# The first FFN chunks' low weight halves on VectorE instead of GpSimd, and half of the last layer norm's first token block on VectorE

## The chip, the core and the metric

The kernel runs on one core of one Trainium2 chip. A core has TensorE (PE, matmuls into eight PSUM banks), VectorE (DVE), ScalarE (ACT), GpSimd (POOL) and SyncE (SP, which here issues nearly all DMAs). Each engine works through its own instructions in a fixed order and waits on semaphores for what others deliver. The metric is the time of one execution in microseconds, the median of several.

## The reference

One decoder block, 512 tokens of 1024 channels, fp32: three sub-layers, each with its input shifted and scaled, and its output gated, by vectors computed from a conditioning vector c; each ends in a layer norm over the residual sum.

```python
mod = (silu(c) @ w_ada + b_ada).reshape(9, D)
sh1, sc1, g1, sh2, sc2, g2, sh3, sc3, g3 = mod
u = x * (1 + sc1) + sh1
x = layer_norm(ALPHA * x + g1 * (0.5 * swiglu(u, w_gu1, w_down1)), ln1_g, ln1_b)
u = x * (1 + sc2) + sh2
x = layer_norm(ALPHA * x + g2 * mixing(u), ln2_g, ln2_b)
u = x * (1 + sc3) + sh3
x = layer_norm(ALPHA * x + g3 * (0.5 * swiglu(u, w_gu2, w_down2)), ln3_g, ln3_b)
```

`swiglu` is `(silu(a) * g) @ w_down` with `a, g` the halves of `u @ w_gu` (2 x 2816 columns). `mixing` is stick-breaking attention beside a gated depthwise convolution. The change touches the start of the first FFN (`sc1`, `sh1`, `u`, and the first 8 of the 44 column tiles of `w_gu1`) and the last layer norm.

## The kernel before

Every fp32 matmul is done as three fp32r products: a matrix is split into a high part (a cast, `whi`, `uh`) and a low part (what the cast leaves, `wlo`, `ul`), and whi x uh, whi x ul and wlo x uh are summed in PSUM. Weights arrive as tiles of 128 x 1024 (512 KB). Such a tile is loaded into one of 3 slots named `raw`, ScalarE casts it to `whi` (L112), and another engine writes `wlo = raw - whi` (L113) into one of 5 slots; in most of the kernel that engine is GpSimd, in the down projections and two tiles of the second FFN it is VectorE. A slot of `raw` is free again when `wlo` is made, slots of `whi` and `wlo` when TensorE has read them.

The first FFN begins in `first_group`, because `u` is not there yet: the scale and shift vectors come from `silu(c) @ w_ada`. The loop runs over 8 chunks k of 128 input channels. Per chunk it loads one tile of x transposed (`xT`, 256 KB), four tiles of ada weights (256 KB each) and one `raw` tile (L100). VectorE multiplies each ada tile by `crow` (silu(c) on all partitions) and sums it along its columns in one instruction (`column_sums`, L188); reduces the four sums to a scale and a shift per channel, `m` (L448, L449). ScalarE makes `uf = xT * scale + shift` (L454; for k = 0 VectorE does, L452). VectorE casts `uf` to `uh` (L456) and subtracts for `ul` (L457). TensorE then does 8 x 3 matmuls of 128 x 512, one set of three for each of 8 PSUM banks (L460, L461, L464), where the eight banks hold the a and g halves of FFN columns 0 to 3. After chunk 7 the rest of the FFN follows, tiles h4a, h4g, h5a and so on, 24 matmuls each (L143 to L145), with their weights' `wlo` on GpSimd. Meanwhile VectorE works off background tasks in its gaps (further gate, scale and shift vectors, L188, L221).

A scheduler of the language decides the order of instructions on each engine from the order of the code and its own estimate of time; `keep_in_program_order` fixes the order among the instructions given to it. `load(..., True)` keeps the first loads in the order of the code on SP's queue. The loads of SP use eight semaphores in turn, so a load is issued only when the one eight places before it has landed.

The last layer norm (`layer_norm_out`) runs per block t of 128 tokens while TensorE still works on the later blocks. `residual_stats` adds PSUM and x (L260) and takes the statistics (L261, L263, L265) on VectorE, and GpSimd makes `rstd` (L267). The rest is done in one of two ways, for the last `dve_from` channels and for the others: ScalarE normalises (L334, with a bias `shift` from L333) and GpSimd multiplies by g and adds b (L335, L336); or VectorE does both in two instructions (L340, L341). `dve_from` is the number of channels that go the way of ScalarE and GpSimd: 1024 for t = 0, 512 for t = 1 and 2, none for t = 3.

Of the kernel before, what the change touches and what calls it, by code (L numbers as in the profile page):

```python
# [25 lines left out]
SEG = 2  # L26
# [16 lines left out]
def decoder_block(ctx: ExitStack, tc: tile.TileContext, a: dict, out: bass.AP):  # L43
    nc = tc.nc

    core = ctx.enter_context(tc.tile_pool(name="core", bufs=1))
    wts = ctx.enter_context(tc.tile_pool(name="wts", bufs=1))
# [16 lines left out]
    def bank(name, tag="ps"):  # L64
        return banks["pool"].tile([P, 512], F32, tag=tag, name=name, bufs=banks["bufs"][tag])
# [21 lines left out]
    b0pair = vec[:, 0:16].rearrange("p (c two) -> p c two", two=2)  # L87
# [11 lines left out]
    def load(dst, src, chain=False):  # L99
        ins = nc.sync.dma_start(dst, src).ins  # L100
        if "last" in issued:
            tc.add_manual_dep(ins, issued["last"].name,
                              mybir.DependencyInfo(mybir.DependencyClass.NoSync, mybir.DependencyReason.DATA),
                              reason="first loads in order of use")
        if chain:
            issued["last"] = ins


    def split_w(raw, lo_eng):
        hi = wts.tile([P, 1024], F32R, align_bytes=256, tag="whi", name="whi", bufs=5)  # L110
        lo = wts.tile([P, 1024], F32R, align_bytes=256, tag="wlo", name="wlo", bufs=5)
        nc.scalar.copy(hi, raw)  # L112
        lo_eng.tensor_sub(lo, raw, hi.bitcast(F32))  # L113
        return hi, lo

    def raw_tile(src, chain=False):
        raw = wts.tile([P, 1024], F32, tag="raw", name="raw", bufs=3)
        load(raw, src, chain)
        return raw
# [64 lines left out]
    def column_sums(parts, raw, crow):  # L184
        w = D // SEG
        for q in range(parts.shape[-1]):
            qs = slice(q * w, (q + 1) * w)
            nc.vector.scalar_tensor_tensor(raw[:, qs], raw[:, qs], 1.0, crow[:, qs], ALU.mult, ALU.mult,  # L188
                                           accum_out=parts[:, q : q + 1])
# [135 lines left out]
    def layer_norm_out(pool, t, banks_t, rows):  # L325
        r, mv, rstd = residual_stats(pool, t, banks_t)
        o = core.tile([P, D], F32, tag=f"x{t}", name="o")
        g, b = rows
        dve_from = {0: D, 1: 512, 2: 512}.get(t, 0)
        if dve_from:  # L330
            cs = slice(D - dve_from, D)
            shift = pool.tile([P, 1], F32, tag="shift", name="shift", bufs=2)
            nc.vector.scalar_tensor_tensor(shift, mv[:, 0:1], -1.0, rstd, ALU.mult, ALU.mult)  # L333
            nc.scalar.activation(o[:, cs], r[:, cs], AF.Identity, bias=shift, scale=rstd)  # L334
            nc.gpsimd.tensor_mul(o[:, cs], o[:, cs], g[:, cs])  # L335
            nc.gpsimd.tensor_add(o[:, cs], o[:, cs], b[:, cs])  # L336
            nc.sync.dma_start(out[t * P : (t + 1) * P, cs], o[:, cs])
        for c0 in range(0, D - dve_from, 512):
            cs = slice(c0, c0 + 512)
            nc.vector.scalar_tensor_tensor(o[:, cs], r[:, cs], mv[:, 0:1], g[:, cs], ALU.subtract, ALU.mult)  # L340
            nc.vector.scalar_tensor_tensor(o[:, cs], o[:, cs], rstd, b[:, cs], ALU.mult, ALU.add)  # L341
            nc.sync.dma_start(out[t * P : (t + 1) * P, cs], o[:, cs])
# [83 lines left out]
    crow = lnp.tile([P, D], F32, name="crow")  # L426
# [1 line left out]
    nc.gpsimd.dma_start(vec[:, 0 : 2 * KC], a["vecs"][:, 0 : 2 * KC])  # L428
    nc.scalar.activation(crow, crow, AF.Silu)
    b1 = core.tile([P, KC, 2], F32, name="b1")  # L430
    nc.vector.tensor_scalar_add(b1[:, :, 0:1], b0pair[:, :, 0:1], 1.0)
    nc.vector.tensor_copy(b1[:, :, 1:2], b0pair[:, :, 1:2])

    def first_group(gated, fp):
        pss = [bank(f"first{i}") for i in range(NFIRST)]
        uh, ul = u1
        for k in range(KC):
            parts = fp.tile([P, 2, SEG], F32, tag="parts0", name="parts0", bufs=2)
            xc = fp.tile([P, S], F32, tag="sF", name="xT", bufs=NF)
            load(xc, a["xT"][k], True)  # L440
            for x in range(2):
                for h in range(2):
                    rt = fp.tile([P, S], F32, tag="sF", name="ada0", bufs=NF)
                    hs = slice(h * 512, (h + 1) * 512)
                    load(rt, a["ada0"][k, x, :, hs], True)
                    column_sums(parts[:, x, h * SEG // 2 : (h + 1) * SEG // 2], rt, crow[:, hs])
            m = fp.tile([P, 2], F32, tag="m0", name="m0", bufs=2)
            nc.vector.tensor_reduce(m, parts, mybir.AxisListType.X, ALU.add)  # L448
            nc.vector.tensor_add(m, m, b1[:, k, :])  # L449
            uf = fp.tile([P, S], F32, tag="sF", name="uf0", bufs=NF)  # L450
            if k == 0:
                nc.vector.tensor_scalar(uf, xc, m[:, 0:1], m[:, 1:2], ALU.mult, ALU.add)  # L452
            else:
                nc.scalar.activation(uf, xc, AF.Identity, bias=m[:, 1:2], scale=m[:, 0:1])  # L454
            wh, wl = split_w(raw_tile(a["gu1_first"][k], True), nc.gpsimd)
            nc.vector.tensor_copy(uh[:, k, :], uf)  # L456
            nc.vector.tensor_sub(ul[:, k, :], uf, uh[:, k, :].bitcast(F32))  # L457
            for i, ps in enumerate(pss):
                cs = slice(i * P, (i + 1) * P)
                nc.tensor.matmul(ps, wh[:, cs], uh[:, k, :], start=(k == 0), stop=False)  # L460
                nc.tensor.matmul(ps, wh[:, cs], ul[:, k, :], start=False, stop=False)  # L461
# [32 lines left out]
    def begin1(gated, fp):  # L494
        return first_group(gated, fp)
# [483 lines left out]
```

## Time and profile before

| | us |
|---|---|
| median of 3 runs | 1330.25 (1327.76 to 1333.49) |
| the profiled execution | 1328.88 |
| its span (first to last instruction) | 1327.2 |
| first matmul of the first group | 11.37 |
| first matmul of h4a, behind the first group | 66.84 |
| TensorE busy | 1292.2 |
| VectorE, ScalarE, GpSimd busy | 750.8, 524.6, 559.7 |

The rows of the trace that are shown further down read: start in us from the span's start, duration in us, engine, line, operation, out<-in with their shapes, number of instructions in a row of the same kind, and in brackets how long the engine sat idle before it and what ended that wait. Matmuls overlap on TensorE, so that its pace is the distance between starts, not the duration. For VectorE and ScalarE too, the distance of starts is a little less than the duration when instructions follow each other directly.

### The profile page before, as it was taken

How to read it: one execution, taken by the hardware profiler on the slowest of the kernel's cores; microseconds unless marked ns; L12 is line 12 of the kernel's file. 1: busy time of each engine (PE TensorE's matmuls, PEld its weight loads, DVE VectorE, ACT ScalarE, POOL GpSimd, SP SyncE). 2: the span in 40 equal slices, each digit the busy share in tenths (PEclk: the TensorE clock that was granted, in tenths of full speed). 3: DMA queues.
4: the chain of work that ended last, by engine and by line, in shares of the span. 5: the costliest groups of instructions: out<-in, count | busy, mean ns of one | idle time of the engine just before them, and what ended most of it. 6: DMA issues, size and time to landing. Idle time of an engine off the chain costs nothing.

```text
span 1327.2 us, 16780 instructions
## 1 busy us (share of the span) xinstructions
PE 1292.2 (97%) x6444; PEld 1071.2 (81%) x6444; DVE 750.8 (57%) x1017; ACT 524.6 (40%) x794; POOL 559.7 (42%) x392
## 2 busy tenths in 40 slices
PE   6899999999999999999999999999999999999997
PEld 4688888888889878788778888878898888888885
DVE  7886885255462858766676876545672000025545
ACT  2233312222256555556556444852542222222220
POOL 2464535644222554534442111133264566564434
PEclk9999999999999989999999999999999999999999
DMA  9668886333327564655566989293273333323311
GB/s 356 217 211 314 293 293 215 103 96 96 95 81 171 123 150 96 159 112 118 121 135 135 191 193 200 51 225 109 77 272 100 101 106 101 117 96 96 96 64 63
DMA packets 57713, 197.36 MB, mean 149 GB/s; under 512 B 6673, under 2 KB 6817, under 8 KB 57633
## 3 DMA queue, kind: packets, MB, share of 16 engines
q1 hardware_dynamic: 47808, 160.63, 36.6%
q0 software_dynamic: 9824, 35.66, 16.4%
q8 instruction: 50, 0.82, 0.2%
q14 instruction: 31, 0.25, 0.1%
HBM read 194.17 MB, written 2.10 MB: 148 GB/s over the span
## 4 chain that ended last, share of the span: by engine, by line
PE 84%; DVE 8%; DMA 3%; issue 2%; ACT 1%; POOL 1%; SPq 0%; DVEq 0%; POOLq 0%; ACTq 0%
PE y L354 19%; DVE ada L188 3%; PE z L624 1%; DVE cacc L525 1%; PE pw L646 1%; PE glub L143 1%; PE ga L143 1%; PE ga L145 1%; PE ysb L145 1%; PE ga L144 1%; PE ysb L144 1%; PE ysb L143 1%; PE q L143 1%; PE glub L144 1%; PE glub L145 1%
## 5 line engine op out<-in xcount | busy, mean ns | idle before, releaser
L113 POOL TENSOR_TENSOR wlo<-raw,whi 128x1024 fp32r<-128x1024 f32 x88 | 224.8, 2561 | 239.0 <-ACT whi L112 233.5
L112 ACT CAST whi<-raw 128x1024 fp32r<-128x1024 f32 x144 | 149.6, 1046 | 265.3 <-DMA raw<-in_gu 45.2
L136 POOL TENSOR_TENSOR raw<-raw,mod_g 128x1024 f32<-128x1024 f32 x52 | 130.0, 2502 | 146.9 <-DMA raw<-in_dn 83.7
L525 DVE SCALAR_TENSOR_TENSOR cacc<-h,cv_w,cacc 128x512 f32<-128x512 f32 x232 | 179.7, 833 | 0.0
L129 ACT CAST whi<-raw 128x1024 fp32r<-128x1024 f32 x68 | 71.1, 1048 | 129.1 <-PE ysb L144 23.4
L113 DVE TENSOR_TENSOR wlo<-raw,whi 128x1024 fp32r<-128x1024 f32 x56 | 106.2, 1896 | 24.2 <-ACT whi L112 24.2
L354 PE MATMUL y<-whi,sh 128*128 128x512 f32 x352 | 113.8, 390 | 0.0
L354 PE MATMUL y<-wlo,sh 128*128 128x512 f32 x352 | 113.7, 389 | 0.0
L354 PE MATMUL y<-whi,sl 128*128 128x512 f32 x352 | 113.6, 389 | 0.0
L188 DVE SCALAR_TENSOR_TENSOR ada<-ada,crow 128x512 f32<-128x512 f32 x96 | 97.9, 1067 | 20.9 <-DMA ada<-in_ada_t 15.4
L418 DVE TENSOR_TENSOR sl<-sF,sh 128x512 fp32r<-128x512 f32 x44 | 45.3, 1031 | 85.3 <-ACT sh L417 85.3
L417 ACT CAST sh<-sF 128x512 fp32r<-128x512 f32 x44 | 27.1, 623 | 144.9 <-PE y L354 132.1
L131 POOL DMA_DIRECT2D wlo<-in_w_in x44 | 38.4, 872 | 98.9 <-ACT wlo L130 92.9
L636 POOL TENSOR_TENSOR be<-be,nb 128x127 f32<-128x127 f32 (+1 forms) x64 | 50.1, 783 | 68.7 <-DVE nb L631 55.1
L354 PEld LDWEIGHTS y<-whi,sl 128*128 128x128 f32 x352 | 66.1, 188 | 13.7
L354 PEld LDWEIGHTS y<-wlo,sh 128*128 128x128 f32 x352 | 66.1, 188 | 13.7
L354 PEld LDWEIGHTS y<-whi,sh 128*128 128x128 f32 x352 | 66.1, 188 | 13.5
L130 ACT ACTIVATE wlo<-whi 128x1024 fp32r<-128x1024 f32 x68 | 71.9, 1061 | 0.7
L650 DVE TENSOR_TENSOR wTl<-pw,wTh 128x128 fp32r<-128x128 f32 (+1 forms) x64 | 31.1, 485 | 52.8 <-ACT wTh L649 52.7
L634 POOL TENSOR_SCALAR_AFFINE_SELECT be<-be 128x128 f32<-128x128 f32 x64 | 40.9, 639 | 41.0 <-ACT be L630 40.6
L631 DVE TENSOR_TENSOR_SCAN nb<-nb,future 128x127 f32<-128x127 f32 (+1 forms) x64 | 53.4, 835 | 3.4 <-ACT nb L629 3.4
L221 DVE SCALAR_TENSOR_TENSOR acc<-ada,silu_c,acc 128x1024 f32<-128x1024 f32 x21 | 41.6, 1981 | 15.8 <-DMA ada<-in_ada_w 15.6
(494 smaller groups left out, 3376.4 us busy)
## 6 DMA issues: line engine op xcount, KB each, us to landing
raw<-in_gu SPq DMA_DIRECT2D x80, 512.0 KB, 3.6
raw<-in_w_in SPq DMA_DIRECT2D x48, 512.0 KB, 3.6
raw<-in_dn SPq DMA_DIRECT2D x44, 512.0 KB, 3.5
wlo<-in_w_in POOLq DMA_DIRECT2D x44, 512.0 KB, 6.0
ada<-in_ada_t SPq DMA_DIRECT2D x32, 512.0 KB, 5.3
ada<-in_ada_w SPq DMA_DIRECT2D x24, 512.0 KB, 5.0
ada<-in_ada SPq DMA_DIRECT2D x32, 256.0 KB, 6.0
raw<-in_gu_first SPq DMA_DIRECT2D x8, 512.0 KB, 6.6
```

The costliest lines, as they stand in the source:

```text
L112: nc.scalar.copy(hi, raw)
L113: lo_eng.tensor_sub(lo, raw, hi.bitcast(F32))
L129: nc.scalar.copy(hi, raw)
L130: nc.scalar.mul(lo, hi.bitcast(F32), -1.0)
L136: nc.gpsimd.tensor_mul(raw, raw, G)
L143: nc.tensor.matmul(ps[:, c0:c1], wh[:, ks], mov(uh, k)[:, c0:c1], start=(k == 0), stop=False)
L188: nc.vector.scalar_tensor_tensor(raw[:, qs], raw[:, qs], 1.0, crow[:, qs], ALU.mult, ALU.mult, accum_out=parts[:, q : q + 1])
L354: nc.tensor.matmul(acc[t][h][:, c0 - h * 512 : c1 - h * 512], st[:, tsl], wt[:, c0:c1], start=(k == 0 and i == 0 and c0 % 512 == 0), stop= ...
L418: nc.vector.tensor_sub(sl, sF[f], sh.bitcast(F32))
L525: ins = nc.vector.scalar_tensor_tensor(o, hv, cv_w[:, j, i : i + 1], o, ALU.mult, ALU.add)
L631: nc.vector.tensor_tensor_scan(nb[:, 1:n][:, ::-1], nb[:, 1:n][:, ::-1], future[:, S - n + 1 : S][:, ::-1], 1.0, ALU.mult, ALU.max)
L636: nc.gpsimd.tensor_mul(be[:, 0 : n - 1], be[:, 0 : n - 1], nb[:, 1:n])
```

## The change

In `first_group` the loop body is written anew. `wlo` of the eight chunks is made by VectorE (L473, and L477 for chunk 0) and no longer by GpSimd. The load of `raw` stands ahead of the four ada loads for k > 0. The cast to `whi` (L455) comes before the ada sums in the code and thereby before `uf` on ScalarE. `column_sums` is written out with one 512-column sum per tile, as before. All these instructions are given to `keep_in_program_order`. The two small instructions on `b1` move into the loop. The matmuls are unchanged. In `layer_norm_out`, `dve_from` for t = 0 is 512 and no longer 1024, as for t = 1 and 2.

```diff
-        dve_from = {0: D, 1: 512, 2: 512}.get(t, 0)
+        dve_from = {0: 512, 1: 512, 2: 512}.get(t, 0)
...
         for k in range(KC):
             parts = fp.tile([P, 2, SEG], F32, tag="parts0", name="parts0", bufs=2)
             xc = fp.tile([P, S], F32, tag="sF", name="xT", bufs=NF)
             load(xc, a["xT"][k], True)
+            raw = None if k == 0 else raw_tile(a["gu1_first"][k], True)
...
+            if k == 0:
+                raw = raw_tile(a["gu1_first"][k], True)
+            wh = wts.tile([P, 1024], F32R, align_bytes=256, tag="whi", name="whi", bufs=5)
+            wl = wts.tile([P, 1024], F32R, align_bytes=256, tag="wlo", name="wlo", bufs=5)
+            if k:
+                in_turn(nc.scalar.copy(wh, raw))
+            for x in range(2):
+                for h in range(2):
+                    rt = rts[2 * x + h]
+                    in_turn(nc.vector.scalar_tensor_tensor(rt, rt, 1.0, crow[:, h * 512 : (h + 1) * 512], ALU.mult,
+                                                           ALU.mult, accum_out=parts[:, x, h : h + 1]))
             m = fp.tile([P, 2], F32, tag="m0", name="m0", bufs=2)
-            nc.vector.tensor_reduce(m, parts, mybir.AxisListType.X, ALU.add)
-            nc.vector.tensor_add(m, m, b1[:, k, :])
+            in_turn(nc.vector.tensor_reduce(m, parts, mybir.AxisListType.X, ALU.add))
...
+            in_turn(nc.vector.tensor_add(m, m, b1[:, k, :]))
             uf = fp.tile([P, S], F32, tag="sF", name="uf0", bufs=NF)
             if k == 0:
-                nc.vector.tensor_scalar(uf, xc, m[:, 0:1], m[:, 1:2], ALU.mult, ALU.add)
+                in_turn(nc.vector.tensor_scalar(uf, xc, m[:, 0:1], m[:, 1:2], ALU.mult, ALU.add))
+                in_turn(nc.scalar.copy(wh, raw))
             else:
-                nc.scalar.activation(uf, xc, AF.Identity, bias=m[:, 1:2], scale=m[:, 0:1])
-            wh, wl = split_w(raw_tile(a["gu1_first"][k], True), nc.gpsimd)
-            nc.vector.tensor_copy(uh[:, k, :], uf)
-            nc.vector.tensor_sub(ul[:, k, :], uf, uh[:, k, :].bitcast(F32))
+                in_turn(nc.scalar.activation(uf, xc, AF.Identity, bias=m[:, 1:2], scale=m[:, 0:1]))
+                in_turn(nc.vector.tensor_sub(wl, raw, wh.bitcast(F32)))
+            in_turn(nc.vector.tensor_copy(uh[:, k, :], uf))
+            in_turn(nc.vector.tensor_sub(ul[:, k, :], uf, uh[:, k, :].bitcast(F32)))
+            if k == 0:
+                in_turn(nc.vector.tensor_sub(wl, raw, wh.bitcast(F32)))
```

VectorE's instructions at chunk 1, before (`ada0`, `parts0`, `m0`, `uf0` are the tiles of this loop; the number behind a name tells one buffer from another):

```order
L457 TENSOR_TENSOR ul_80<-uf0_120,uh_79 128x512
L188 SCALAR_TENSOR_TENSOR ada0_157,parts0_154<-ada0_157,crow_84 128x512
L188 SCALAR_TENSOR_TENSOR ada0_160,parts0_154<-ada0_160,crow_84 128x512
L188 SCALAR_TENSOR_TENSOR ada0_163,parts0_154<-ada0_163,crow_84 128x512
L188 SCALAR_TENSOR_TENSOR ada0_166,parts0_154<-ada0_166,crow_84 128x512
L448 TENSOR_REDUCE m0_169<-parts0_154 128x2
L449 TENSOR_TENSOR m0_169<-m0_169,b1_88 128x2
L456 CAST uh_79<-uf0_172 128x512
L457 TENSOR_TENSOR ul_80<-uf0_172,uh_79 128x512
```

And at the same place in the changed kernel, from `ul` of chunk 0 on:

```order
L475 TENSOR_TENSOR ul_80<-uf0_124,uh_79 128x512
L477 TENSOR_TENSOR wlo_114<-raw_111,whi_113 128x1024
L459 SCALAR_TENSOR_TENSOR ada0_159,parts0_154<-ada0_159,crow_84 128x512
L459 SCALAR_TENSOR_TENSOR ada0_161,parts0_154<-ada0_161,crow_84 128x512
L459 SCALAR_TENSOR_TENSOR ada0_163,parts0_154<-ada0_163,crow_84 128x512
L459 SCALAR_TENSOR_TENSOR ada0_165,parts0_154<-ada0_165,crow_84 128x512
L462 TENSOR_REDUCE m0_174<-parts0_154 128x2
L466 TENSOR_TENSOR m0_174<-m0_174,b1_88 128x2
L473 TENSOR_TENSOR wlo_168<-raw_157,whi_167 128x1024
L474 CAST uh_79<-uf0_177 128x512
L475 TENSOR_TENSOR ul_80<-uf0_177,uh_79 128x512
```

Chunk 0's `wlo` now stands ahead of chunk 1's sums; from chunk 1 on, `wlo` stands between `m` and `uh`.

SP's loads from chunk 0's `raw` to chunk 2's `xT`, before:

```order
L100 DMA raw_122<-in_gu1_first 128x1024
L100 DMA xT_155<-in_xT 128x512
L100 DMA ada0_157<-in_ada0 128x512
L100 DMA ada0_160<-in_ada0 128x512
L100 DMA ada0_163<-in_ada0 128x512
L100 DMA ada0_166<-in_ada0 128x512
L100 DMA raw_174<-in_gu1_first 128x1024
L100 DMA xT_207<-in_xT 128x512
```

And now:

```order
L100 DMA raw_111<-in_gu1_first 128x1024
L100 DMA xT_155<-in_xT 128x512
L100 DMA raw_157<-in_gu1_first 128x1024
L100 DMA ada0_159<-in_ada0 128x512
L100 DMA ada0_161<-in_ada0 128x512
L100 DMA ada0_163<-in_ada0 128x512
L100 DMA ada0_165<-in_ada0 128x512
L100 DMA xT_207<-in_xT 128x512
```

Chunk 1's `raw` has moved ahead of its four ada tiles; the same holds for every later chunk.

VectorE at the last layer norm, token blocks 0 and 1, from block 0's statistics on (`o` is the output tile, `r` the residual sum), before:

```order
L265 TENSOR_SCALAR ve_10661<-mv_10659 128x1
L333 SCALAR_TENSOR_TENSOR shift_10666<-mv_10659,rstd_10663 128x1
L260 TENSOR_TENSOR r_10696<-y10_9945,n1_8178 128x512
L261 BN_STATS st_10697<-r_10696 128x6
L260 TENSOR_TENSOR r_10696<-y11_9946,n1_8178 128x512
```

And now:

```order
L265 TENSOR_SCALAR ve_10661<-mv_10659 128x1
L340 SCALAR_TENSOR_TENSOR o_10665<-r_10653,mv_10659,lng_10649 128x512
L333 SCALAR_TENSOR_TENSOR shift_10666<-mv_10659,rstd_10663 128x1
L341 SCALAR_TENSOR_TENSOR o_10665<-o_10665,rstd_10663,lnb_10651 128x512
L260 TENSOR_TENSOR r_10699<-y10_9945,n1_8178 128x512
L261 BN_STATS st_10700<-r_10699 128x6
L260 TENSOR_TENSOR r_10699<-y11_9946,n1_8178 128x512
```

Two operations on half of block 0 stand ahead of block 1's first sum; on ScalarE and GpSimd block 0's three operations (L334, L335, L336) go from 128 x 1024 to 128 x 512.

More of the change, by code (lines that the diff above doesn't have):

```diff
@@ L430, in decoder_block @@
     b1 = core.tile([P, KC, 2], F32, name="b1")
-    nc.vector.tensor_scalar_add(b1[:, :, 0:1], b0pair[:, :, 0:1], 1.0)
-    nc.vector.tensor_copy(b1[:, :, 1:2], b0pair[:, :, 1:2])
     def first_group(gated, fp):
@@ L436, in first_group, with in_turn @@
         uh, ul = u1
+        def in_turn(ins):
+            tc.keep_in_program_order(ins)
         for k in range(KC):
@@ L440, in first_group @@
             load(xc, a["xT"][k], True)
+            raw = None if k == 0 else raw_tile(a["gu1_first"][k], True)
+            rts = []
             for x in range(2):
@@ L443, in first_group @@
                     rt = fp.tile([P, S], F32, tag="sF", name="ada0", bufs=NF)
-                    hs = slice(h * 512, (h + 1) * 512)
-                    load(rt, a["ada0"][k, x, :, hs], True)
-                    column_sums(parts[:, x, h * SEG // 2 : (h + 1) * SEG // 2], rt, crow[:, hs])
-            m = fp.tile([P, 2], F32, tag="m0", name="m0", bufs=2)
-            nc.vector.tensor_reduce(m, parts, mybir.AxisListType.X, ALU.add)
-            nc.vector.tensor_add(m, m, b1[:, k, :])
+                    load(rt, a["ada0"][k, x, :, h * 512 : (h + 1) * 512], True)
@@ new lines, in first_group @@
+                    rts.append(rt)
+            if k == 0:
[9 more added lines that the diff above has]
+                                                           ALU.mult, accum_out=parts[:, x, h : h + 1]))
@@ L450, in first_group @@
+            m = fp.tile([P, 2], F32, tag="m0", name="m0", bufs=2)
+            in_turn(nc.vector.tensor_reduce(m, parts, mybir.AxisListType.X, ALU.add))
+            if k == 0:
+                in_turn(nc.vector.tensor_scalar_add(b1[:, :, 0:1], b0pair[:, :, 0:1], 1.0))
+                in_turn(nc.vector.tensor_copy(b1[:, :, 1:2], b0pair[:, :, 1:2]))
+            in_turn(nc.vector.tensor_add(m, m, b1[:, k, :]))
             uf = fp.tile([P, S], F32, tag="sF", name="uf0", bufs=NF)
             if k == 0:
-                nc.vector.tensor_scalar(uf, xc, m[:, 0:1], m[:, 1:2], ALU.mult, ALU.add)
-            else:
-                nc.scalar.activation(uf, xc, AF.Identity, bias=m[:, 1:2], scale=m[:, 0:1])
@@ L458, in first_group @@
+            in_turn(nc.vector.tensor_copy(uh[:, k, :], uf))
+            in_turn(nc.vector.tensor_sub(ul[:, k, :], uf, uh[:, k, :].bitcast(F32)))
+            if k == 0:
+                in_turn(nc.vector.tensor_sub(wl, raw, wh.bitcast(F32)))
             for i, ps in enumerate(pss):
```

## The prediction

> **What bounds the kernel now.** I read the page's busy times first, then who TensorE waited for, then the first chunks instruction by instruction, then the end of the chain.
>
> ```profile
> PE 1292.2 (97%) x6444; PEld 1071.2 (81%) x6444; DVE 750.8 (57%) x1017; ACT 524.6 (40%) x794; POOL 559.7 (42%) x392
> ```
> ```profile
> PE first L460 <- ACT whi L112: 18.3, 7, 11.4
> PE ycv L145 <- DMA wlo<-in_w_cv: 2.9, 1, 2.9
> ```
>
> TensorE is busy 97% of the span, so only its idle time can be won. The table of TensorE's waits (total, times, longest) puts 18.3 us of it on the first chunks: 11.4 before the first matmul, 6.9 in six later waits. Nothing else there exceeds 2.9 us. One chunk of the first eight, on all engines:
>
> ```profile
> 46.13 0.43 DVE L456 CAST uh<-uf 128x512 fp32r<-128x512 f32 x1 [0.88 <-ACT uf L454]
> 46.59 0.69 DVE L457 TENSOR_TENSOR ul<-uf,uh 128x512 fp32r<-128x512 f32 x1
> 47.11 2.43 POOL L113 TENSOR_TENSOR wlo<-raw,whi 128x1024 fp32r<-128x1024 f32 x1 [4.64 <-ACT whi L112]
> 47.20 2.89 DVE L188 SCALAR_TENSOR_TENSOR ada<-ada,crow 128x512 f32<-128x512 f32 x1
> 50.02 0.68 DVE L188 SCALAR_TENSOR_TENSOR ada<-ada,crow 128x512 f32<-128x512 f32 x1
> 50.63 0.68 DVE L188 SCALAR_TENSOR_TENSOR ada<-ada,crow 128x512 f32<-128x512 f32 x1
> 51.97 0.16 DVE L448 TENSOR_REDUCE m<-parts 128x2 f32<-128x4 f32 x1
> 52.16 0.16 DVE L449 TENSOR_TENSOR m<-m,b 128x2 f32<-128x2 f32 x1
> 53.20 0.43 DVE L456 CAST uh<-uf 128x512 fp32r<-128x512 f32 x1 [0.88 <-ACT uf L454]
> ```
>
> From one uh cast (46.13) to the next (53.20) is 7.07 us. The first column sum takes 2.82 us to the second, the second 0.61 to the third: 2.21 us in which it stands until GpSimd's wlo (47.11 to 49.54) is over. The wait for ScalarE's uf costs 0.88 more. VectorE's chain sets the period. TensorE's own pace:
>
> ```profile
> 13.03 0.63 PE L461 MATMUL first<-ul,whi 128*128 128x512 f32 x1
> 13.46 0.63 PE L460 MATMUL first<-uh,whi 128*128 128x512 f32 x1
> 17.30 0.48 PE L461 MATMUL first<-ul,whi 128*128 128x512 f32 x1
> 19.92 0.39 PE L460 MATMUL first<-uh,whi 128*128 128x512 f32 x1
> 25.87 0.50 PE L460 MATMUL first<-uh,whi 128*128 128x512 f32 x1 [0.35 <-ACT whi L112]
> 66.84 0.39 PE L143 MATMUL h4a<-uh,whi 128*128 128x512 f32 x1
> 72.28 0.39 PE L143 MATMUL h4g<-uh,whi 128*128 128x512 f32 x1
> ```
>
> A tile of 24 matmuls takes 72.28 - 66.84 = 5.44 us (0.227 each). Chunk 0 runs at half pace (0.43 a step) until 17.30. Chunk 1 starts at 19.92 and TensorE first waits at 25.87: up to there it is the bound already. From 19.92 to 66.84 it needs 46.92 us for seven chunks, worth 7 x 5.44 = 38.08. At most **8.84 us** can be won here (6.9 of waits, the rest slower steps after each wait).
>
> **The wlo of the first chunks, moved to VectorE.** Eight GpSimd subtractions go, eight VectorE ones come. The last stage has their price without GpSimd beside them; the group's mean over the kernel is with it:
>
> ```profile
> 1286.69 1.22 DVE L113 TENSOR_TENSOR wlo<-raw,whi 128x1024 fp32r<-128x1024 f32 x1 [0.26 <-ACT whi L112]
> L113 DVE TENSOR_TENSOR wlo<-raw,whi 128x1024 fp32r<-128x1024 f32 x56 | 106.2, 1896 | 24.2 <-ACT whi L112 24.2
> ```
>
> GpSimd is idle in this stage, so 1.22; the bounds are 1.22 and 2.43, GpSimd's own time. For k > 0 the new wlo stands between m and the uh cast, where VectorE idles 0.88. From m to uh it was 1.04; now 0.19 (the step of such a small operation) + 1.22 = 1.41, so +0.37. The stall of 2.21 goes. Period: 7.07 - 2.21 + 0.37 = **5.23 us**, under TensorE's 5.44. Chunk by chunk VectorE gains 0.21 on TensorE.
>
> The head start must hold too.
>
> ```profile
> 11.87 2.85 DVE L188 SCALAR_TENSOR_TENSOR ada<-ada,crow 128x512 f32<-128x512 f32 x1
> 17.60:25.80 8.20, 7.92 (x35) 6.20 (x33) 6.94 (x14) 2.88 (x4) 2.42 (x1) 1.00 1.04 391
> ada<-in_ada SPq DMA_DIRECT2D x32, 256.0 KB, 6.0
> raw<-in_gu_first SPq DMA_DIRECT2D x8, 512.0 KB, 6.6
> ```
>
> VectorE is through with ul of chunk 0 at 11.87; wlo of chunk 0 puts the column sums of chunk 1 at 13.09. From the first sum to m is 52.16 - 47.20 - 2.21 = 2.75, so m at 15.84 and uh at 17.25. TensorE wants it at 19.92: 2.67 us of cover. With wlo at 1.90 the cover shrinks by 1.36 and the period is 5.91, so chunk 7 would be 2.67 - 1.36 - 6 x 0.47 = 1.5 us late.
>
> **Loads.** A chunk brings 256 + 4 x 256 + 512 KB = 1.835 MB; at the window's 391 GB/s (last column) that is 4.69 us, under 5.44. No bytes are added. raw now goes ahead of the four ada loads on SP, which delays these by 512 KB, 1.34 us; the sums of chunk 1 are at the same time held to 13.09, so I charge nothing (bound 1.3, inside the cover). Behind a raw that waits for its slot now stand ada of the same chunk and everything later on SP. Of three slots, raw(k) needs wlo(k-3), which is done at 13.09 for k = 3, at 17.25 for k = 4, then every 5.23: earlier than GpSimd's.
>
> **The casts and matmuls.** ScalarE's whi moves ahead of uf (about 1 us each, over 4 us idle per chunk): free. uf of chunk 7 now stands behind silu_c, which waits for cvec; 7 x 4.69 after chunk 0's raw (10.2) that lands near 44, and m of chunk 7 comes at 15.84 + 6 x 5.23 = 47.2: free. TensorE does four uh products before four ul ones: the same 24.
>
> **Hand-over to h4a.** All stages behind start 8.84 earlier, and their weights must too.
>
> ```profile
> 61.26 5.25 POOL L113 TENSOR_TENSOR wlo<-raw,whi 128x1024 fp32r<-128x1024 f32 x2 [4.64 <-ACT whi L112]
> 68.53 2.40 POOL L113 TENSOR_TENSOR wlo<-raw,whi 128x1024 fp32r<-128x1024 f32 x1 [2.02 <-ACT whi L112]
> 213.29 2.39 POOL L113 TENSOR_TENSOR wlo<-raw,whi 128x1024 fp32r<-128x1024 f32 x1 [5.71 <-ACT whi L112]
> 226.55 0.39 PE L143 MATMUL h18g<-uh,whi 128*128 128x512 f32 x1
> ```
>
> Before, h4a's wlo ended at 66.51, 0.33 us ahead of its first matmul. Now GpSimd has nothing before it. whi of h4a follows uf(7), near 48, wlo ends near 51.5 and h4g's near 54: over 6 us before 58.0. h5a's whi now stands behind four sh casts on ScalarE; with everything 8.84 earlier its wlo ends near 65 and is wanted at 58.0 + 10.88 = 68.9: about 3.7 us of cover, gone if the casts slip by more. Later, h18g's wlo ends at 215.68, 10.9 us ahead of TensorE: even a chain that did not move at all would leave 2.0.
>
> **The last layer norm.** Half of token block 0 leaves ScalarE and GpSimd for VectorE (two operations of 0.74).
>
> ```profile
> 1301.86 0.69 DVE L260 TENSOR_TENSOR r<-y,n 128x512 f32<-128x512 f32 x1 [1.30 <-PE y L354]
> 1307.30 0.69 DVE L260 TENSOR_TENSOR r<-y,n 128x512 f32<-128x512 f32 x1 [1.30 <-PE y L354]
> 1308.38 2.40 POOL L336 TENSOR_TENSOR o<-o,lnb 128x1024 f32<-128x1024 f32 x1
> 1309.07 2.27 DVE L340 SCALAR_TENSOR_TENSOR o<-r,mv,lng 128x512 f32<-128x512 f32 x1
> 1310.75 1.00 POOL L267 TENSOR_TENSOR rstd<-ve,mhalf 128x1 f32<-128x1 f32 x1
> 1312.53 0.68 DVE L260 TENSOR_TENSOR r<-y,n 128x512 f32<-128x512 f32 x1
> 1318.86 0.67 DVE L260 TENSOR_TENSOR r<-y,n 128x512 f32<-128x512 f32 x1
> ```
>
> GpSimd works on block 0 until 1310.78; block 1's rstd waits for that and VectorE's L340 stands beside it. VectorE stays behind: block 3's last sum starts at 1318.86, though TensorE, 5.44 a block after 1301.86 and 1307.30, delivers it at 1318.18. With halves (about 1.3 each, as for blocks 1 and 2) GpSimd is free near 1308.1, rstd of block 1 runs at 1309.2, and block 2's first sum starts near 1311 instead of 1312.53. VectorE then waits for TensorE in block 3. Gain 1318.86 - 1318.18 = **0.68**; bounds 0 and 0.68. The two added operations fill VectorE's wait of 1.30 ahead of 1307.30.
>
> **Sum.** The profiled execution took 1328.88 (span 1327.2 + 1.68 around it): 1328.88 - 8.84 - 0.68 = 1319.4. The median before is 1330.25, 1.37 higher; minus 9.52 that gives 1320.7. I take the middle, **1320.0**.
>
> **Rivals.**
>
> *An even exchange* (0.10). VectorE pays in work what it lost in waiting. For it: if wlo cost GpSimd's 2.43, the period would be 6.44 and uh(1) 19.67; chunk 7 would start at 58.3, not 52.6, leaving 3.1 of 8.84, so 1325.1 on the profiled run; at 1.90 it is 1320.9. Against it: 1.22 in the row above. The Trainium skill, "Perfetto Trace Analysis", Optimizing Scalar/DVE Operations, says that moving work between GpSimd and VectorE might not help, since they share a read port; this trace has 2.21 of stall against 0.37 of lengthening, and so disagrees here.
>
> *Another length of the half-paced start* (0.10). Chunks 0 and 1 were already back to back on TensorE, but an earlier full pace would only have lengthened the wait at 25.87; now it counts. 14 matmuls went at 0.43; six fewer would save 6 x 0.2 = 1.2: 1318.2. The Trainium skill, "TensorE: Matmul & The Clock Gate", What's actually happening, gives about 3.4 us of busy time in free-running windows; the trace shows 5.9, from 11.37 to 17.30, so the moment may move.
>
> *The gain is lost behind* (0.12). h5a's weights miss their 3.7 us of cover, or the weights of the rest of the FFN fall back more than the 2.0 that I left. Each us beyond is a us lost: 1324 to 1329. For it: both are shorter than before; against it: their own inputs come earlier too.
>
> *SP blocks itself, slower* (0.04). raw(k) waits for wlo(k-3) with ada(k) behind it, and ada(k) feeds wlo(k): a loop over three chunks of about 6.6 (landing) + 1.7 (issues) + 4.2 (sums to wlo) = 12.5 us, 4.2 a chunk. It is slower than before only when the loop passes 3 x 7.07 = 21.2, that is when landing takes 15 us and not 6.6. At 20 us it is 8.6 a chunk, seven times 1.6 more: 1340.
>
> *My forecast*: 0.64.
>
> **Range and chances.** The three runs before spread from 2.5 below their median to 3.2 above. Low end: 1318.2 less some scatter, **1316.5**; high end: the even exchange at 1325.1, **1325.5**. Left out are most of the lost gain and the blocked queue. 0.5% (6.65 us, about what a measurement can tell from no change) is passed below 1323.6: 0.64 + 0.10 + 0.06 of the exchange + 0.02 of the lost gain = 0.82; within 0.14; slower 0.04.
>
> **What would show it.** In the changed profile: no wait of "first" matmuls but the first; h4a's first matmul near 58.0; uh casts 5.2 us apart; column sums of 0.61 without a long first; wlo on VectorE at 1.2; block 3's last sum waiting for TensorE. It is wrong if sums wait for ada loads, if wlo takes over 1.9, or if h4a to h5g wait for weights.

## The result and the profile after

The changed kernel takes 1315.72 us, the median of 6 runs (1314.33 to 1316.71). Three more runs of the kernel before, taken beside them, lie lower than the first three (1326.33, 1326.39, 1327.31), so that its median over six is 1327.53. The ratio is 0.9902, with a 95% interval of 0.9883 to 0.9922. The change is a gain, as forecast, and the time lies 0.8 us below the low end of the range.

| us | before | after | difference |
|---|---|---|---|
| the profiled execution | 1328.88 | 1316.71 | -12.2 |
| its span | 1327.2 | 1315.0 | -12.2 |
| first matmul of h4a | 66.84 | 57.44 | -9.40 |
| from there to the start of the last matmul | 1250.91 | 1249.49 | -1.42 |
| from there to the end of the span | 9.42 | 8.08 | -1.34 |

The page's busy times and the table of TensorE's waits (total, times, longest), of the changed kernel:

```profile
PE 1288.2 (98%) x6444; PEld 1070.0 (81%) x6444; DVE 747.8 (57%) x1027; ACT 524.9 (40%) x794; POOL 540.9 (41%) x384
```
```profile
PE first L480 <- ACT whi L470: 11.3, 1, 11.3
PE ycv L145 <- DMA wlo<-in_w_cv: 3.3, 1, 3.3
PE po L689 <- ACT wTh L669: 1.7, 1, 1.7
PE po L690 <- DVE wTl L670: 1.0, 2, 0.6
PE ga L143 <- ACT h L584: 0.7, 1, 0.7
PE h0a L144 <- DVE ul L292: 0.7, 1, 0.7
```

"first" waits once, ahead of its first matmul, and the six later waits are gone. One chunk on VectorE, in the timeline of the changed kernel:

```profile
41.02 0.16 DVE L466 TENSOR_TENSOR m<-m,b 128x2 f32<-128x2 f32 x1
41.13 1.22 DVE L473 TENSOR_TENSOR wlo<-raw,whi 128x1024 fp32r<-128x1024 f32 x1
42.27 0.42 DVE L474 CAST uh<-uf 128x512 fp32r<-128x512 f32 x1
...
43.34 0.68 DVE L459 SCALAR_TENSOR_TENSOR ada<-ada,crow 128x512 f32<-128x512 f32 x1
...
43.95 0.69 DVE L459 SCALAR_TENSOR_TENSOR ada<-ada,crow 128x512 f32<-128x512 f32 x1
...
47.34 0.42 DVE L474 CAST uh<-uf 128x512 fp32r<-128x512 f32 x1
```

The long first sum is gone: 43.34 to 43.95 is 0.61. `wlo` takes 1.22, nothing waits, and from one uh cast to the next is 5.07 here; from 17.00 to 47.34 six periods average 5.06, where 5.23 was forecast. The same stage on TensorE and GpSimd:

```profile
15.97 0.54 PE L480 MATMUL first<-uh,whi 128*128 128x512 f32 x1
16.35 0.40 PE L481 MATMUL first<-ul,whi 128*128 128x512 f32 x1
...
19.36 1.07 PE L480 MATMUL first<-uh,whi 128*128 128x512 f32 x4
...
57.44 0.39 PE L143 MATMUL h4a<-uh,whi 128*128 128x512 f32 x1
```
```profile
48.41 5.21 POOL L113 TENSOR_TENSOR wlo<-raw,whi 128x1024 fp32r<-128x1024 f32 x2 [45.70 <-ACT whi L112]
61.22 3.21 POOL L113 TENSOR_TENSOR wlo<-raw,whi 128x1024 fp32r<-128x1024 f32 x1 [7.59 <-ACT whi L112]
```

From 19.36 to 57.44 is 38.08, seven chunks at 5.44 without a gap: TensorE sets the pace. Half pace ends in the row at 15.97 (0.38 to the next start, then 0.24), while the kernel before kept it until 17.30; so chunk 1 starts 0.56 earlier, and h4a's 9.40 is 8.84 and 0.56. The hand-over holds: h4a's and h4g's `wlo` are done at 53.62, h5a's at 64.43, against 68.3 when TensorE wants it. Its cast to `whi` (at 60.07) stands behind the four sh casts that begin at 57.99, as foreseen.

The end, VectorE and SP's queue with the time from issue to landing of the last store (the last figure of the `out<-o SPq` rows, in us), of the kernel before, and then of the changed one:

```profile
1321.93 1.41 DVE L341 SCALAR_TENSOR_TENSOR o<-o,rstd,lnb 128x512 f32<-128x512 f32 x2
1322.70 1.08 SPq L342 DMA_DIRECT2D out<-o  x2
```
```profile
out<-o SPq DMA_DIRECT2D x1, 256.0 KB, 2.6
```
```profile
1307.36 0.69 DVE L260 TENSOR_TENSOR r<-y,n 128x512 f32<-128x512 f32 x1 [0.33 <-PE y L354]
...
1310.45 1.41 DVE L341 SCALAR_TENSOR_TENSOR o<-o,rstd,lnb 128x512 f32<-128x512 f32 x2
1311.22 0.99 SPq L342 DMA_DIRECT2D out<-o  x2
```
```profile
out<-o SPq DMA_DIRECT2D x1, 256.0 KB, 2.0
```

Block 3's last sum (1307.36) now waits for TensorE; it starts 0.43 us after the last matmul's start at 1306.93 instead of 1.10. That is the forecast 0.67. The span ends 3.16 us after VectorE (1311.85 to 1315.01) instead of 3.84 (1323.34 to 1327.18): another 0.68, which no step of the prediction had. Most of it is the last store, which lands 2.0 us after its issue instead of 2.6.

The middle, where nothing was changed, became 1.42 us shorter. A table by stretches (busy time and instructions of PE, PEld, DVE, ACT and POOL, then the granted clock, the DMA share and GB/s) of the kernel before, then the changed one:

```profile
480.00:510.00 30.00, 27.49 (x148) 21.21 (x147) 16.54 (x25) 13.21 (x26) 14.60 (x18) 0.89 0.55 122
```
```profile
470.00:500.00 30.00, 27.82 (x154) 21.35 (x153) 17.24 (x26) 14.74 (x28) 15.51 (x19) 0.94 0.55 124
```

In these stretches, and in one more near 870 and 860 us, TensorE was granted half its clock for a while. Before, these half-paced stretches were 6.83 us (from 488.5) and 3.41 us (from 870.8), 10.24 in all; after, 3.41 us twice. Half pace loses about half its length (0.43 us a step instead of 0.23), so the difference of 3.42 is worth about 1.71. Less half of the half-paced time and less TensorE's waits in between (2.9, 2.1, 1.3, 0.7 and 0.3 before, 3.3, 1.7, 1.0, 0.7 and 0.7 after), the middle is 1250.91 - 5.12 - 7.3 = 1238.5 before and 1249.49 - 3.41 - 7.4 = 1238.7 after: the same. Whether the change has a part in the stretches is a question for the experiments.

### The profile page after: what moved, and what is told of

The parts are those of the page before. It is cut to its first block, busy times and chain, and to the rows that moved or that the text cites. A ratio compares the mean times of both kernels' runs of the same rounds, so it can differ in the third digit from the quotient of the medians.

```text
span 1315.0 us, 16764 instructions
## 1 busy us (share of the span) xinstructions
PE 1288.2 (98%) x6444; PEld 1070.0 (81%) x6444; DVE 747.8 (57%) x1027; ACT 524.9 (40%) x794; POOL 540.9 (41%) x384
## 4 chain that ended last, share of the span: by engine, by line
PE 92%; DVE 3%; DMA 2%; issue 2%; ACT 0%; SPq 0%; POOL 0%; DVEq 0%; POOLq 0%; ACTq 0%
PE y L354 21%; PE z L644 2%; PE psv L620 1%; PE pw L666 1%; PE q L143 1%; PE glub L143 1%; PE first L480 1%; PE first L481 1%; PE psv L621 1%; PE psv L622 1%; PE glua L143 1%; PE ga L143 1%; PE ysb L145 1%; PE ysb L143 1%; PE ga L145 1%
## 5 line engine op out<-in xcount | busy, mean ns | idle before, releaser
L113 POOL TENSOR_TENSOR wlo<-raw,whi 128x1024 fp32r<-128x1024 f32 x80 | 204.5, 2562 | 254.2 <-ACT whi L112 253.1
L112 ACT CAST whi<-raw 128x1024 fp32r<-128x1024 f32 x136 | 141.9, 1047 | 272.5 <-DMA raw<-in_gu 47.7
L136 POOL TENSOR_TENSOR raw<-raw,mod_g 128x1024 f32<-128x1024 f32 x52 | 132.7, 2555 | 140.5 <-DMA raw<-in_dn 80.5
L129 ACT CAST whi<-raw 128x1024 fp32r<-128x1024 f32 x68 | 71.1, 1048 | 129.3 <-PE ysb L144 23.4
L188 DVE SCALAR_TENSOR_TENSOR ada<-ada,crow 128x512 f32<-128x512 f32 x64 | 70.0, 1141 | 12.2 <-DMA ada<-in_ada_t 12.2
```

The costliest lines, as they stand in the source:

```text
L136: nc.gpsimd.tensor_mul(raw, raw, G)
```

## The experiments

My theory was that GpSimd's `wlo` held VectorE's column sum, and that the exchange (2.21 of stall for less than 0.4) put VectorE below TensorE's pace. The rivals were that the new order did it without the move, that a faster engine alone did it without the new order, that the load order did it, and, for the surplus over the forecast, the half-paced start, the half-paced stretches in the middle, and the last stores.

### One part of the change at a time, and both kernels again

**first_only** is the changed kernel with the last layer norm of before:

```diff
-        dve_from = {0: 512, 1: 512, 2: 512}.get(t, 0)
+        dve_from = {0: D, 1: 512, 2: 512}.get(t, 0)
```

> The first group as changed, the last layer norm as before. If the parts are independent (the sum of the prediction), h4a starts near 57.4 as in the changed kernel, block 3's last sum starts 0.7 us late again, and the time is 9 to 10 us under the kernel before (ratio 0.9925 to 0.993). If the two parts need each other, or the last stage gave more than the 0.68 predicted, it is clearly less: a gain of 8 or under (0.994 or more).

**tail_only** is the kernel before with the changed layer norm (the reverse of that edit).

> The first group as before, the last layer norm as changed. By the prediction 0.68 us under the kernel before (ratio 0.9995), h4a at 66.8. If the end behind block 3's last sum gained too, as the two spans of before and after suggest (0.70 more), 1.4 us (0.999). If the time from 480 to 970 us is better for a reason of the last stage's code, 2 us or more (0.9985).

**before_again** and **after_again** are the two kernels, without an edit, on the same chip.

> The kernel before, unchanged, for a second trace of it. If the 1.4 us that the changed kernel gained net between h4a and the last stage are a matter of how many half-paced stretches of TensorE an execution meets, this trace shows another number or other lengths of them than 6.8 us at 488 and 3.4 us at 871, and its first full pace comes at another moment than 17.4. If they belong to the change, it shows the same again to 0.3 us.

> The changed kernel, unchanged, for a second trace of it. If the half-paced stretches vary by execution, the span differs from 1315.0 by about 1.7 us for every stretch of 3.4 us more or less; if they belong to the change, 3.4 us at 480 and 3.4 us at 859 again and a span within 0.5 us.

| us | time | ratio to before, 95% | h4a | h4a to last matmul | last matmul to end | VectorE's end to span's end | half-paced in the middle |
|---|---|---|---|---|---|---|---|
| first_only | 1316.56 | 0.9929 (0.9912 to 0.9946) | 57.36 | 1249.36 | 8.84 | 3.27 | 6.83 |
| tail_only | 1325.90 | 0.9995 (0.9984 to 1.0005) | 66.62 | 1251.33 | 8.07 | 3.15 | 10.24 |
| before_again | 1328.32 (one run) | | 66.64 | 1250.56 | 9.41 | 3.86 | 10.24 |
| after_again | 1315.25 (one run) | | 57.12 | 1248.35 | 8.08 | 3.16 | 6.82 |

The median before, on this chip, is 1326.07 (17 runs). The first group alone brings 9.5 us of it, 0.7% with an interval of 0.5 to 0.9%. The layer norm alone brings 1.35 us in the traces' last stage, but its time can't be told from no change (0.05% faster, interval from 0.16% faster to 0.05% slower). So nearly all of the gain is the first group's, and the effect of the layer norm on the time rests on traces. Together the parts come to 9.7 us here, less than the 11.8 between the medians of the first comparison, whose six runs of the kernel before include the high 1330.25 and 1333.49. The last sum waits for TensorE in tail_only as in the changed kernel, so that this step doesn't depend on the first group. The last 0.68 us, from VectorE's end to the span's, is less clear: with the changed layer norm this stretch is 3.15 to 3.19 in all nine traces of this study, with the old one 3.73 to 3.86 in four and 3.27 in first_only. The last store lands 2.5 to 2.6 us after its issue in the three traces of the kernel before and 2.0 to 2.1 us in all others, first_only among them, so the old layer norm alone does not make it slow; in vector_old_order some 0.5 us more follow the landing instead. What decides it is open.

The two traces without an edit fit neither side of their expectations fully. In before_again the half-paced stretches came in the other order (3.41 us from 489.5, 6.83 from 868.4), with the same sum, and full pace came at 15.03 instead of 17.44 (within the matmul that starts at 17.30). after_again had 3.41 us twice again, but its span is 1.46 us shorter than that of the first trace; 1.14 of this lies in the middle, where TensorE waited 6.0 us instead of 7.4.

### Which part of the first group

**gpsimd_new_order** is the changed kernel with `wlo` back on GpSimd, everything else in the new order:

```diff
-                in_turn(nc.vector.tensor_sub(wl, raw, wh.bitcast(F32)))
+                nc.gpsimd.tensor_sub(wl, raw, wh.bitcast(F32))
```

> The changed kernel with wlo of the eight chunks back on GpSimd; loads, casts and fixed order stay as changed. If the stall of VectorE beside GpSimd's wlo set the period, it is back: a column sum of about 2.8 us in every chunk, uh casts 6.2 to 7.1 us apart, h4a between 62 and 67. If the new order of loads and casts brought the gain, the uh casts stay 5.1 to 5.4 us apart and h4a stays near 57.5.

It takes 1326.08 us (one run; before on the same chip 1327.64). TensorE's waits behind its first matmul, and one chunk on VectorE and GpSimd:

```profile
PE first L480 <- DVE uh L474: 8.5, 7, 1.4
```
```profile
40.89 0.43 DVE L474 CAST uh<-uf 128x512 fp32r<-128x512 f32 x1 [0.88 <-ACT uf L472]
...
41.96 2.90 DVE L459 SCALAR_TENSOR_TENSOR ada<-ada,crow 128x512 f32<-128x512 f32 x1
...
44.79 0.68 DVE L459 SCALAR_TENSOR_TENSOR ada<-ada,crow 128x512 f32<-128x512 f32 x1
...
47.97 0.43 DVE L474 CAST uh<-uf 128x512 fp32r<-128x512 f32 x1 [0.88 <-ACT uf L472]
```
```profile
41.87 2.43 POOL L473 TENSOR_TENSOR wlo<-raw,whi 128x1024 fp32r<-128x1024 f32 x1 [4.65 <-ACT whi L455]
```

With GpSimd's `wlo` (41.87 to 44.30) the long first sum is back: 2.83 us to the next start instead of 0.61. The period is 7.08 (40.89 to 47.97) as before, TensorE waits in all seven chunks, and h4a comes at 68.20, 1.4 us later than before and beyond the 67 that was expected. So the order alone brings nothing, and the stall is the cause. The Trainium skill, "SBUF — State Buffer", Who interferes with whom, says that a VectorE instruction with two inputs in SBUF contends with a GpSimd one that reads SBUF; the row at 41.96, whose follower starts only 0.5 us after GpSimd's end, agrees.

**vector_old_order** is the kernel before with only the engine changed:

```diff
-            wh, wl = split_w(raw_tile(a["gu1_first"][k], True), nc.gpsimd)
+            wh, wl = split_w(raw_tile(a["gu1_first"][k], True), nc.vector)
```

> The kernel before with wlo of the eight chunks on VectorE and nothing else changed; wlo then stands behind ul and whi behind uf. If the stall was the cause and wlo's place in the wait for uf counts only for the rest, the period is 4.86 + 1.15 = 6.0 us, above TensorE's 5.44, and h4a starts near 59.4: some 2 us behind the changed kernel, 7.4 ahead of before. If the place and the fixed order do most of it, h4a is above 63.

It takes 1321.15 us (one run). TensorE's only wait for the first group, and VectorE in its first chunks:

```profile
PE first L460 <- DVE uh L456: 13.8, 1, 13.8
```
```profile
11.01 1.23 DVE L113 TENSOR_TENSOR wlo<-raw,whi 128x1024 fp32r<-128x1024 f32 x1 [1.47 <-ACT whi L112]
...
13.20 0.43 DVE L456 CAST uh<-uf 128x512 fp32r<-128x512 f32 x1
...
18.07 0.43 DVE L456 CAST uh<-uf 128x512 fp32r<-128x512 f32 x1 [0.88 <-ACT uf L454]
...
19.14 1.22 DVE L113 TENSOR_TENSOR wlo<-raw,whi 128x1024 fp32r<-128x1024 f32 x1
...
24.08 0.43 DVE L456 CAST uh<-uf 128x512 fp32r<-128x512 f32 x1 [0.88 <-ACT uf L454]
```

The period is 6.01: `wlo` stands behind `ul`, and the wait of 0.88 for `uf` stays open. That is above TensorE's 5.44, and yet TensorE, contrary to the expectation, shows no wait behind its first matmul. In chunk 0 the scheduler put `wlo` ahead of `b1` and the second step of `m`, where VectorE waited 1.47 us for `whi`; the first uh cast is at 13.20 instead of 10.8, and the first matmul at 13.78 instead of 11.4. TensorE therefore reaches chunk 1 only at 22.39, 3.9 us after that chunk's `uh` is ready, and this cover shrinks by some 0.57 a chunk to 0.5 us at chunk 7. h4a comes at 60.67, not at the 59.4 that was expected: of the 3.2 us behind the changed kernel 2.4 are the later first matmul and 0.8 what follows, 0.6 of it a longer chunk 0. So the move to VectorE alone brings 6.2 us of the 9.4, and the new order as a whole, chunk 0 included, 3.2. What `wlo`'s place in the wait for `uf` is worth by itself, this run does not separate: with chunk 7's `uh` ready at 54.56, VectorE would have held h4a near 60 even behind an earlier first matmul (an estimate, 54.6 + 5.5).

**double_wlo** is the changed kernel with each of the eight subtractions done twice, which adds one more to the period:

```diff
                 in_turn(nc.vector.tensor_sub(wl, raw, wh.bitcast(F32)))
+                in_turn(nc.vector.tensor_sub(wl, raw, wh.bitcast(F32)))
```

> The changed kernel with every wlo of the first eight chunks made twice on VectorE. The period becomes 5.05 + 1.14 = 6.19 us, above TensorE's 5.44; the cover of 2.36 us at chunk 1 is used up by chunk 2, chunk 7 starts near 56.4 and h4a near 61.9, 4.4 us later than the changed kernel. If something else than VectorE's chain or TensorE's pace sets h4a's start, it stays near 57.4.

It takes 1327.89 us (one run). TensorE's waits, VectorE's chunk, then what happened at chunk 7, and the stretch from 58 to 66 us in the table by stretches:

```profile
PE first L482 <- DVE uh L475: 6.3, 7, 2.7
```
```profile
38.09 0.42 DVE L475 CAST uh<-uf 128x512 fp32r<-128x512 f32 x1
...
42.02 1.22 DVE L473 TENSOR_TENSOR wlo<-raw,whi 128x1024 fp32r<-128x1024 f32 x1
43.28 1.22 DVE L474 TENSOR_TENSOR wlo<-raw,whi 128x1024 fp32r<-128x1024 f32 x1
44.42 0.42 DVE L475 CAST uh<-uf 128x512 fp32r<-128x512 f32 x1
```
```profile
56.62 5.27 POOL L113 TENSOR_TENSOR wlo<-raw,whi 128x1024 fp32r<-128x1024 f32 x2 [53.91 <-ACT whi L112]
57.09 2.57 DVE L475 CAST uh<-uf 128x512 fp32r<-128x512 f32 x1
...
59.71 2.73 PE L482 MATMUL first<-uh,whi 128*128 128x512 f32 x6 [2.73 <-DVE uh L475]
```
```profile
58.00:66.00 8.00, 5.64 (x13) 3.95 (x14) 5.04 (x3) 0.00 (x0) 3.89 (x2) 0.62 0.72 238
```

The period is 6.33 (expected 6.19), so VectorE is the bound again and TensorE waits in every chunk: the second `wlo` adds its 1.22 to the period, and the first one's price is on the path as soon as TensorE's 5.44 is passed. But h4a comes at 69.03 and not at 61.9. The expectation missed two things. Behind two `wlo`, the uh cast of chunk 7 came so late that GpSimd's `wlo` of h4a and h4g (from 56.62) ran beside it, and it took 2.57 us instead of 0.42: chunk 7 starts at 59.71 and not near 56.4, 3.3 us late, 2.1 of this by the cast. And from 59.96 on, right behind that wait of 2.73 us, TensorE was granted half its clock for 6.83 us (a mean of 0.62 in the last row): with 0.65 more of waiting for `ul`, chunk 7 takes 9.3 us instead of 5.5, another 3.8. So the stall came back by another pair of instructions.

**raw_last** is the changed kernel with `raw` loaded behind the four ada tiles, as before:

```diff
-            raw = None if k == 0 else raw_tile(a["gu1_first"][k], True)
...
-            if k == 0:
-                raw = raw_tile(a["gu1_first"][k], True)
+            raw = raw_tile(a["gu1_first"][k], True)
```

> The changed kernel with raw loaded behind the ada tiles of its chunk, as before. If the engine that makes wlo is what counts, and loads keep ahead of VectorE, h4a stays at 57.1 to 57.5 and the uh casts 5.05 apart. If raw's place is needed, whi of chunk 1 comes later than 15.9 and h4a later by 1 us or more.

It takes 1315.79 us (one run), the period is 5.05 and h4a comes at 57.13, all within what the changed kernel shows. The place of `raw` in SP's queue makes no difference.

### The half-paced start

**warm_30** puts 30 matmuls of 128 columns ahead of the first group, into a bank that the group overwrites:

```diff
+        for _ in range(30):
+            nc.tensor.matmul(pss[-1][:, :P], ones_r, ones_r, start=True, stop=True)
```

> The changed kernel with 30 matmuls of 128 x 128 on a tile of ones ahead of the first real matmul, in a bank that is written anew afterwards; their results are used nowhere. If TensorE's half pace at the start depends on its work just before, chunk 0 runs at 0.227 us a step from 11.4 on, chunk 1 starts near 17.1 (uh of chunk 1 is ready at 17.0) and h4a near 55.2: 2.2 us under the changed kernel. If the half pace goes with the first real matmuls whatever ran before, or the 30 matmuls are not over at 11.3, h4a stays at 57.4 or later.

It takes 1319.16 us (ratio 0.9935, 0.9922 to 0.9949; the changed kernel has 0.9902, 0.9883 to 0.9922). TensorE at its start:

```profile
1.51 6.66 PE L436 MATMUL first<-ones_r 128*128 128x128 f32 x30 [1.51 <-DVE ones_r L78]
11.17 0.76 PE L482 MATMUL first<-uh,whi 128*128 128x512 f32 x1 [3.00 <-ACT whi L472]
...
17.09 0.44 PE L483 MATMUL first<-ul,whi 128*128 128x512 f32 x1
```

6.66 us of narrow matmuls without a gap did not lift the pace: it is half until about 17.2, 6.0 us after the first wide matmul, and h4a comes at 57.72. **warm_wide** does it with 24 matmuls of 512 columns that reach up to the first real one:

```diff
+        wide = lnp.tile([P, 512], F32R, name="wide")
+        for i in range(4):
+            nc.vector.tensor_copy(wide[:, i * P : (i + 1) * P], ones)
+        for _ in range(24):
+            nc.tensor.matmul(pss[-1], ones_r, wide, start=True, stop=True)
```

> As warm_30, but 24 matmuls of 128 x 512, which fill TensorE more than the 128 x 128 ones (those took 0.222 us each, and the clock stayed at half for all of them). At half pace they last from 2.5 to at most 12.7 us. If steady wide work for one or two windows of 3.4 us brings the full pace, the clock rises before 10 us, chunk 0 runs at 0.227 us a step, h4a starts near 55.2 and the time is 2.2 us under the changed kernel, 13 under the kernel before (ratio 0.990). If the pace is bound to something else, h4a stays at 57.1 or later, and the time at the changed kernel's.

TensorE's busy time by stretches, and its first chunk, in warm_wide:

```profile
2.20:8.10 5.90, 5.87 (x14) 4.62 (x15) 1.40 (x5) 1.06 (x1) 0.51 (x1) 1.00 0.96 320
8.10:10.80 2.70, 2.64 (x12) 1.80 (x10) 2.56 (x10) 0.87 (x1) 0.00 (x0) 1.00 1.03 413
```
```profile
12.29 0.39 PE L486 MATMUL first<-ul,whi 128*128 128x512 f32 x1
12.52 0.40 PE L485 MATMUL first<-uh,whi 128*128 128x512 f32 x1
...
17.22 1.20 PE L485 MATMUL first<-uh,whi 128*128 128x512 f32 x4
```

14 matmuls in 5.9 us (0.42 each), then 12 in 2.7 (0.22): the pace was full from 8.1 on (the column of the granted clock reads 1.00 in both rows, because its record begins only there), so chunk 0 ran at 0.23 a step and chunk 1 began at 17.22 instead of 19.36. h4a comes at 55.45 (expected 55.2), 1.0 to 2.0 us earlier than in the changed kernel's traces. That shows what the start costs. The time doesn't show it: 1317.19 us (ratio 0.992, 0.9907 to 0.9933), and the stretch from h4a to the last matmul is 1252.09, with 10.24 us of half pace and 1.5 us of a new wait of the q projection. So it is no better than the changed kernel.

### The middle, once more

**before_3** and **after_3** are the two kernels again, on a third chip.

> A third trace of the kernel before. Two traces had 10.2 us of half pace between h4a and the last matmul. If their number is a matter of the execution, 6.8 or 13.7 can come; if it belongs to the kernel, 10.2 again. In either case the stretch from h4a to the last matmul, less half of the half-paced time, less TensorE's waits in it, is 1238.6 to 0.3 us as in the two others.

> A third trace of the changed kernel. Two traces had 6.8 us of half pace between h4a and the last matmul. If a matter of the execution, 10.2 or 3.4 can come; if it belongs to the kernel, 6.8 again. The same stretch, less half of that and less the waits, is again 1238.6 to 0.3 us.

before_3: 1327.95 us, h4a at 66.83, 10.24 us of half pace in the middle, 1250.03 from h4a to the last matmul. after_3: 1318.00 us, h4a at 56.40, 10.24 us of half pace, 1251.83. Less half of the half pace and TensorE's waits (6.9 and 7.8), that is 1238.0 and 1238.9: the second is within the 0.3 that was expected, the first 0.3 outside it. The changed kernel, in after_3, by stretches:

```profile
465.00:495.00 30.00, 27.42 (x144) 20.99 (x143) 16.94 (x23) 13.77 (x25) 17.52 (x20) 0.89 0.57 125
```

This is the 0.89 of the kernel before. So the changed kernel has the longer stretch in some executions too. In the traces the split is still uneven: 10.24 in all four with the first group of before as it was, 6.83 in four of five with the changed first group (first_only and raw_last counted), and an effect of the change on its frequency isn't excluded. The five other variants show both: 6.83 in gpsimd_new_order and vector_old_order, 10.24 in double_wlo (besides its stretch at 60 us), warm_30 and warm_wide. The times allow a fairer comparison, since each run comes with its mean granted clock. It is a rough measure: the half pace at the start is not in it, while 3 to 6 us at half clock behind the last matmul, which cost nothing, are. Means of the 41 runs of before that were taken with the experiments and the 8 of the changed kernel:

| mean granted clock | before (runs) | changed (runs) | difference, us |
|---|---|---|---|
| 0.994 | 1328.08 (14) | 1318.00 (1) | 10.1 |
| 0.995 | 1326.77 (10) | 1316.26 (2) | 10.5 |
| 0.996 | 1326.05 (10) | 1315.30 (5) | 10.7 |

The kernel before goes from 1330.57 at 0.993 (3 runs) to 1323.73 at 0.997 (4 runs): its 7 us of scatter follow the clock. At the same clock the change is worth 10.1 to 10.7 us; between the medians of all these runs (1327.09 and 1315.72) it is 11.4.

## Why the prediction was wrong in its number and right in its mechanism

The time lies outside the range because the sum started from too high a level and because two of its terms, the first group and the last stage, came out too small.

**The stall and the period: right.** GpSimd's `wlo` set the period (gpsimd_new_order brings 7.08 back), VectorE's own `wlo` costs 1.22, and the period falls below TensorE's 5.44. The 1.41 from `m` to `uh` came out as 1.25 (41.02 to 42.27), which only adds to the cover. The cover itself was counted to the start of the uh cast; TensorE can begin only at the cast's end, 0.4 us later (17.42 for a wanted 19.36); the price of the even exchange has the same slip, and nothing here hung on it. The rival of an even exchange fell with it.

**"At most 8.84 us can be won here": too small.** The bound was worked out from chunk 1 on and took its start at 19.92 as given. The sizes measured are 9.40 in the profiled pair, and 9.2 to 10.4 between any trace of before (66.64 to 66.84) and any of the changed kernel (56.40 to 57.44). The rest is the rival of the half-paced start, whose mechanism the runs bear out. Before, the moment of full pace was swallowed by TensorE's next wait: in the four traces with the old group it came 3.6 to 6.1 us after the first matmul, and h4a stands 55.5 us behind that matmul in all four, to within 0.03. Now it counts: in the five with the changed group it came after 3.3, 4.1, 4.6, 5.0 and 5.6 us, and h4a stands 45.31, 45.64, 45.92, 46.11 and 46.38 behind, about half a us for each us of half pace. The prediction gave it 0.10 and left it out of the sum, though the change itself takes away the wait that hid it.

**The hand-over, the loads and the queue: right.** No tile of the first FFN waits for weights, h5a's `wlo` ended at 64.43 (near 65 forecast), no sum waits for an ada load, and raw_last shows that the load order is free. The gain lost behind and the blocked queue did not come.

**The last layer norm: right in its step, mis-sized as a term.** The last sum gained 0.67 (0.68 forecast), but the stage gained 1.34. The bound "0 and 0.68" ended the term at that sum, as if all behind it were fixed; from VectorE's end to the span's end it is not. Most of that is the landing of the last store (2.0 us for 2.6); why it is shorter stays open.

**The sum: the level was off by more than any term.** "I take the middle, 1320.0" rests on a level of 1329.5, from one profiled execution and three runs. The 41 later runs of before have a median of 1327.09: 2.4 of the 4.3 us of the miss. The other 1.9 is the gain, 11.4 between medians for 9.52; in the profiled pair the start (0.56) and the end behind VectorE (0.68) account for 1.2 of this. The rest was not taken apart; at the same granted clock the gain is 10.1 to 10.7 us, so it may lie in the half-paced stretches, which the sum took as fixed. The profiled execution of before had a clock of 0.994, below the 0.995 of the median run, but that could be told only from the later runs: the one slice that reads 8 in its clock row is there in every trace of before.

**The range: too narrow below.** The low end was the rival's 1318.2 less 1.7 of scatter, while the three runs shown differed by 5.7 us. It allowed for a shorter start and some scatter; that the level was 2.4 us lower and the last stage gained 0.68 more came on top.

## What to carry to other kernels

When one engine's instruction holds another, price a move by the stall that goes less the work that comes, and compare the new period with the next engine's pace; where the moved work is put counts too (the new order as a whole brought 3.2 of the 9.4 us here). A period above the next engine's pace costs nothing while the head start lasts (vector_old_order). A stage that becomes TensorE's own lets its half-paced start count, which a later wait used to swallow, so it belongs in the sum. Before a forecast to within 0.5%, take the level from more than a few executions, with their granted clocks, and let the range cover their scatter, here 7 us from 0.993 to 0.997.

## What the runs showed of the hardware

- Full pace came 3.3 us after the first matmul at the earliest (after_3) and 6.3 at the latest (vector_old_order), in traces of kernels that do the same work there. The half-paced stretches in the middle are 3.41 or 6.83 us long in every trace, each beginning late in a wait of TensorE of 1.4 to 3.5 us or up to 3 us behind it. Not every such wait has one: the 1.75 us near 476 in first_only has none. The Trainium skill, "TensorE: Matmul & The Clock Gate", What's actually happening, gives free-running windows of about 3.4 us, of which one busy one lifts the clock; the lengths agree, and the spread lies, to 0.1 us, between one and two such windows.
- 30 matmuls of 128 columns, 0.222 us each and 6.66 us without a gap, did not lift the pace; wide ones of 512 columns did after 5.9 us. There was also a gap of 3.00 us behind the narrow ones and only 0.34 behind the wide ones, and 6.66 us is little more than the 6.3 that other traces took, so whether the width, the gap or the moment decides stays open.
- In double_wlo a single wait of 2.73 us (six others were 0.57 to 0.64) had 6.83 us at half pace right behind it; in gpsimd_new_order seven waits in the same stage, 8.5 us in all and the longest 1.4, had none.
- VectorE's cast of 128 x 512, with one input, took 2.57 us beside a GpSimd `wlo` (double_wlo, 57.09) and 0.42 without, so not only sums with two inputs were held.
